# An attention layer in which the short operands of three kinds of products get zero rows up to 128

## The chip, the core and the metric

One Trainium2 chip, of which the kernel uses one core. The metric is the device time of one execution in microseconds (us); less is better. Engines are named as in the profile: PE is TensorE's matmul, PEld TensorE's weight load, DVE is VectorE, ACT ScalarE, POOL GpSimd, and SP the engine that issues most DMAs.

## What is computed

One inference step of a two-layer decoder for a prompt of 1024 tokens and eight sample sequences of four new tokens each. Layer 0 is a pooling and state-space mixer, layer 1 is attention; each layer ends with a SwiGLU feed-forward part. The change lies in layer 1's attention alone, cut here to what matters:

```python
DILATED_PATTERNS = ((128, 1), (512, 4), (2048, 16))   # (window, dilation)

def mixer_c_prompt(xn, w_qkv, w_o):                   # 1024 tokens, 16 heads of 64
    q, k, v = _split_qkv(xn, w_qkv)
    for window, dil in DILATED_PATTERNS:
        o, lse = dilated_branch_prompt(q, k, v, window, dil)
        ...
    y = _merge_patterns(outs, lses).reshape(b, t, ATT_WIDTH).astype(xn.dtype) @ w_o

def mixer_c_sample(xn, cache_k, cache_v, w_qkv, w_o): # 8 sequences, 4 tokens, 2048 cached rows
    q, k, v = _split_qkv(xn, w_qkv)
    kk = jnp.concatenate([cache_k, k.astype(cache_k.dtype)], axis=1)
    vv = jnp.concatenate([cache_v, v.astype(cache_v.dtype)], axis=1)
    for window, dil in DILATED_PATTERNS:
        idx = buf + jnp.arange(t)[:, None] - dil * jnp.arange(span + 1)[None, :]
        kg, vg = kk[:, idx], vv[:, idx]
        sc = jnp.einsum('bthe,btjhe->bhtj', q, kg, ...) * scale
        p, den, lse = _softmax_stats(sc, valid[None, None])
        o = jnp.einsum('bhtj,btjhe->bthe', p, vg.astype(jnp.float32)) / ...
```

The three patterns are merged into one softmax by the logarithm of the number of patterns that see a distance; that is the mask `strip` (prompt) and `smask` (sample).

## The kernel before

Everything is float32. Most products are made of parts: a value is split into a high part in the reduced type `F32R` and a low part, which is what the high part lacks, and a product is the sum of two or three products of parts (`mm3`, lines 170 to 173). An operand's rows are the partitions over which a product sums. The program is written as a long list of steps. In layer 0 and in the feed-forward parts a scheduler decides their order on each engine; in the two stages of the change (`with tc.manual_schedule()`, lines 1549 and 1933) the order is as written.

**Projections and cached keys (lines 1327 to 1577).** `Project` makes 128 columns of q, k or v from all tokens (lines 171 to 173, 8 times 3 products of 384 or 288 columns for each third of the tokens), and between its groups `keys_slot` handles the 56 tiles of cached keys that the samples look at. For 48 of these tiles `Keys.queries` (line 1453) brings one sample's query rows onto all partitions: two products of 512 columns each with a selector (`selq` or `selh`) as the stationary operand and `qh` as the moving one. `qh` has 64 rows: the high parts of the 32 query rows, then their low parts. ACT or DVE then take the result (lines 1469 and 1472), and POOL or DVE multiply it with the keys.

**Attention (lines 1582 to 1996).** 160 slots, ten for each of the 16 heads, go through a software pipeline that is written out by hand in the loop of line 1941. A slot's steps are:

- PE, `Row.scores` (lines 1838 and 1839): one or two blocks of scores, 128 queries against up to 512 keys. A head's 64 features lie on its own half of the partitions (`own`), and the low part of its queries on the other half (`oth`). The first product takes all 128 rows of `qs` (query high and low parts) against `kh` (the key's high part, on both halves). The second adds the key's low part and takes `own` alone: 64 rows of `qs` against 64 rows of `kl`. There are 12 such pairs in a head, 192 in all: 96 of 512 columns, and 32 each of 384, 256 and 128.
- DVE, `Row.masked` (line 1849): mask and running maximum from PSUM; ACT, `Row.exp` (line 1856), one slot later.
- PE, `Chunk.transposes` (line 1873), six slots after the scores; ACT, `Chunk.hi` (line 1883), and DVE, `Chunk.lo` (line 1890), copy the result into two parts.
- PE, `Chunk.values` (lines 1897 to 1905), two slots after that.
- ACT `fold`, DVE `scale` and `out`, POOL (line 154) at the end of a unit.
- Steps of `Sample`, one of the eight sequences every 20 slots: PE turns its scores and probabilities (lines 1702 to 1705 and 1729 to 1732), and multiplies the probabilities with 16 half tiles of cached values (`product`, lines 1787, 1793, 1794). The last half tile of each eight holds the four new value rows, and its operands have four rows (`rr = TS`): `sw`, and rows 0 to 3 of `hi` and `lo`. ACT and POOL make these parts in `piece` (lines 1772 and 1773, POOL by the helper of line 154).

The buffers between the engines: PSUM banks `s` (3), `pt` (2), `po` (2), `so` (1); SBUF tiles `ph` and `pl` (3 each), `qs`, `kh` and `kl` (2 each: one head is loaded during the other). SP issues all loads of this stage: five for a head (line 1604), and those of cached values (`vpiece`, lines 1650 to 1662), the new rows by line 1662.

Of the kernel before, what the change touches and what calls it, by code (L numbers as in the profile page):

```python
# [18 lines left out]
# order of the steps in the even and odd slots of layer 0's mixer  # L19
ORDER = ("inputs rotate out outputs turn states turn_u scan sums".split(),  # L20
         "inputs rotate mix0 mix1 outputs turn scan mix2 means split".split())
# pieces of the values of the sample, and units of the prompt's queries, whose products are in plain float32
PLAIN_V = (1, 5)
PLAIN_U = 3
P = 128
# [3 lines left out]
NB = 8  # L29
# [3 lines left out]
# token quarters as they are worked on: (first column, number of columns); the second and the last one are  # L33
# followed by the samples' tokens of two steps each
QUARTERS = ((0, 256), (256, 272), (528, 256), (784, 272))
# and their order in the last chunk of the hidden features
# [14 lines left out]
# cached and new positions that one position of the sample looks at  # L51
# [8 lines left out]
def step_kernel(ctx, tc, x_prompt, x_sample, state_pool, state_s5, cache_k, cache_v, norm_gains,  # L60
# [36 lines left out]
    def nm(s):  # L97
        uid[0] += 1
        return f"{s}_{uid[0]}"
# [4 lines left out]
    def linbank():  # L104
        """one bank for products, of the kinds that the phase has to spare"""
        b = banks[-1]
        if not b.kinds:
            return mmbank()
        b.turn += 1
        return dict(m=mmbank, p=tpbank, q=tqbank)[b.kinds[b.turn % len(b.kinds)]]()[:, 0:512]  # L110
# [23 lines left out]
    # ---------------------------------------------------------------- weights  # L134
# [40 lines left out]
    def lin_first(ws, x, consumes):  # L175
        """several output tiles with the token tiles outermost, for an x that is still being made"""
# [17 lines left out]
    # ---------------------------------------------------------------- norms  # L194
# [30 lines left out]
    class Whole:  # L225
        """the features of all tokens in one piece"""
# [13 lines left out]
    class Blocks:  # L240
        """The features as the right-hand sides of seven products of halves (Winograd's form of Strassen's
        algorithm): blocks of half of the features and a quarter of the tokens, for two pairs of quarters, the
        first and the third one, and the second and the last one. Most blocks lie where quarters of y were."""
# [64 lines left out]
    class Boundary:  # L308
        """end of one sub-layer and start of the next for one tile of tokens, in stages"""
# [53 lines left out]
    class Tiles:  # L363
        """takes token tiles as they come; the second half of one overlaps the first half of the next"""
# [72 lines left out]
    class YTiles(Scope):  # L437
        """high and low parts of the features: by quarters of the prompt's tokens, the samples' with the second"""
# [7 lines left out]
        def prompt(self, k, c0=0, c1=SEQ):  # L446
            """(columns of a range of the prompt's tokens, high part, low part)"""
# [6 lines left out]
    # ================================================================ layer 0, mixer  # L454
# [46 lines left out]
    # ---- S5 tables, spilled to DRAM per quarter of 8 groups  # L501
# [32 lines left out]
    # cos and sin of the angle  # L534
# [17 lines left out]
    # powers of lambda_bar, 0..8  # L552
# [27 lines left out]
    # unit phasors e^(i 8 theta 2^k)  # L580
# [9 lines left out]
    # f = (lambda_bar - 1) / lambda ; b_bar = f * b  # L590
# [20 lines left out]
    # bst = [re; im] of b_bar, bss = [im; re]  # L611
# [7 lines left out]
    # c stacks: c1 = [re; -im], c2 = [im; re], columns (g, i)  # L619
# [16 lines left out]
    # h0 of the sample group: h0 = [re; im], h0s = [-im; re], columns (b, g)  # L636
# [16 lines left out]
    for q in range(4):  # L653
# [5 lines left out]
        # V: lambda^(7 - s) b_bar, stacks along the state, columns (g, s, i)  # L659
# [13 lines left out]
        # W: c lambda^k, columns (g, k, i)  # L673
# [11 lines left out]
        # K[d] = Re(c lambda^d b_bar), transposed, with d_skip on d = 0  # L685
# [15 lines left out]
        # E[c] = e^(i 8 theta c), columns (g, c)  # L701
# [24 lines left out]
    # ---- pooling half  # L726
# [9 lines left out]
    class Pool:  # L736
        """a group of the pooling channels, in steps"""
# [11 lines left out]
        def states(self):  # L749
# [6 lines left out]
            # new rows of the buffers  # L756
# [11 lines left out]
        def sums(self):  # L768
            """window sums by doubling"""
# [14 lines left out]
        def means(self):  # L784
            """divide by the count, subtract u"""
# [1293 lines left out]
```

## Time and profile before

| | us |
|---|---|
| median of 3 runs | 2861.05 |
| lowest and highest of them | 2856.1, 2862.39 |
| span of the profiled execution (first to last instruction) | 2854.8 |
| PE busy in it | 2704.5 (95%) |
| DVE, ACT, POOL busy in it | 1705.0, 1125.9, 1406.6 |

No time is listed for the profiled execution beside its span, which is 6.25 us under the median of the runs. Busy shares are means over stages of very different kinds. Times in the views are us from the first instruction. A PE record starts when the product's first column enters, its end is modelled, and records overlap; the time from one start to the next is what a product takes from the engine. "issue" stands for idle time that ends without anything that the profile shows.

### The profile page before, as it was taken

What the parts mean: (1) busy time and instruction counts of PE and PEld (TensorE: products, weight loads), DVE (VectorE), ACT (ScalarE), POOL (GpSimd) and SP (SyncE); (2) the same over time, 40 slices, a digit from 0 to 9 for tenths busy, and PEclk for the clock granted to TensorE, in tenths of its full rate; (3) what the DMA queues carried; (4) which work ended last, traced back from release to release, by engine and by line L of the source; (5) the groups of instructions that cost most, each with busy time, mean ns of one, the idle gap of its engine ahead of it and who ended that gap; (6) DMA issues with size and microseconds to landing.
All of it is one profiled execution on the core that took longest, in us unless ns stands there. A gap on an engine that the chain in (4) does not pass through costs nothing.

```text
span 2854.8 us, 49751 instructions
## 1 busy us (share of the span) xinstructions
PE 2704.5 (95%) x19508; PEld 2525.9 (88%) x19508; DVE 1705.0 (60%) x3117; ACT 1125.9 (39%) x2053; POOL 1406.6 (49%) x998
## 2 busy tenths in 40 slices
PE   7598998999999999899999999999989999999998
PEld 6587997999999999898888666667989999999998
DVE  8777379755552555733333688885497555543555
ACT  4134364322223211523433677775553222233112
POOL 5954456554556443113553455555465545555440
PEclk9798999999999999999999999999989999999999
DMA  5263362222224222525876655554533221223223
GB/s 147 101 202 109 114 196 96 94 78 77 79 83 147 91 91 76 166 105 169 236 201 175 159 145 145 145 145 130 175 117 98 79 83 65 90 92 104 91 91 130
DMA packets 275662, 350.75 MB, mean 123 GB/s; under 512 B 44056, under 2 KB 208668, under 8 KB 275420
## 3 DMA queue, kind: packets, MB, share of 16 engines
q1 hardware_dynamic: 215252, 289.82, 33.9%
q10 hardware_dynamic: 59024, 53.55, 5.6%
q0 software_dynamic: 1152, 4.19, 0.4%
q8 instruction: 154, 2.52, 0.4%
q14 instruction: 80, 0.66, 0.1%
HBM read 268.29 MB, written 79.39 MB: 122 GB/s over the span
## 4 chain that ended last, share of the span: by engine, by line
PE 79%; DVE 9%; issue 5%; DMA 3%; ACT 2%; POOL 2%; SPq 1%; POOLq 0%; ACTq 0%; DVEq 0%
PE pp L172 9%; PE pp L171 9%; PE pp L173 9%; PE mm L171 7%; PE mm L172 7%; PE mm L173 7%; PE pt L1873 3%; PE s L1839 2%; PE tp L172 2%; PE tp L173 2%; PE tp L171 2%; PE tq L171 2%; PE tq L172 2%; PE tq L173 2%; PE s L1838 2%
## 5 line engine op out<-in xcount | busy, mean ns | idle before, releaser
L171 PE MATMUL pp<-blk,whi 128*128 128x272 f32 (+1 forms) x2240 | 638.2, 287 | 9.3 <-DVE ct L1172 6.7
L172 PE MATMUL pp<-blk,wlo 128*128 128x272 f32 (+1 forms) x2240 | 641.1, 288 | 1.9 <-DVE wlo L1141 1.9
L173 PE MATMUL pp<-blk,whi 128*128 128x272 f32 (+1 forms) x2240 | 638.6, 287 | 0.0
L142 POOL TENSOR_TENSOR wlo<-wraw,whi 128x1024 fp32r<-128x1024 f32 x102 | 246.0, 2420 | 575.4 <-ACT whi L141 552.4
L171 PEld LDWEIGHTS pp<-blk,whi 128*128 128x128 f32 x2240 | 425.5, 191 | 10.7 <-DVE ct L1172 7.1
L172 PEld LDWEIGHTS pp<-blk,wlo 128*128 128x128 f32 x2240 | 425.3, 190 | 2.3 <-DVE wlo L1141 2.3
L173 PEld LDWEIGHTS pp<-blk,whi 128*128 128x128 f32 x2240 | 425.5, 190 | 0.0
L1172 DVE TENSOR_TENSOR c<-pp,c 128x528 f32<-128x528 f32 (+1 forms) x308 | 201.7, 656 | 336.6 <-PE pp L173 331.5
L1141 POOL TENSOR_TENSOR wlo<-S,whi 128x1024 fp32r<-128x1024 f32 x90 | 220.6, 2451 | 361.3 <-ACT whi L1140 361.2
L141 ACT CAST whi<-wraw 128x1024 fp32r<-128x1024 f32 x126 | 131.0, 1053 | 363.9 <-PE mm L173 107.3
L1140 ACT CAST whi<-S 128x1024 fp32r<-128x1024 f32 x100 | 105.0, 1050 | 344.2 <-PE pp L173 313.1
L173 PE MATMUL mm<-hid,whi 128*128 128x256 f32 (+1 forms) x680 | 194.5, 286 | 8.1 <-POOL hid L1260 8.1
L171 PE MATMUL mm<-hid,whi 128*128 128x256 f32 (+1 forms) x680 | 197.9, 291 | 1.8 <-DVE yacc L1281 1.8
L172 PE MATMUL mm<-hid,wlo 128*128 128x256 f32 (+1 forms) x680 | 194.5, 286 | 0.0
L171 PE MATMUL mm<-y,whi 128*128 128x256 f32 (+1 forms) x576 | 167.6, 291 | 0.4 <-DVE s5o L1031 0.4
L173 PE MATMUL mm<-y,whi 128*128 128x256 f32 (+1 forms) x576 | 167.0, 290 | 0.0
L172 PE MATMUL mm<-y,wlo 128*128 128x256 f32 (+1 forms) x576 | 166.7, 289 | 0.0
L1281 DVE TENSOR_TENSOR yacc<-mm,yacc 128x272 f32<-128x272 f32 (+1 forms) x264 | 113.1, 430 | 81.5 <-PE mm L173 81.5
L171 PE MATMUL tp<-hid,whi 128*128 128x272 f32 x484 | 138.3, 287 | 0.0
L172 PE MATMUL tp<-hid,wlo 128*128 128x272 f32 x484 | 138.1, 286 | 0.0
L173 PE MATMUL tp<-hid,whi 128*128 128x272 f32 x484 | 137.6, 285 | 0.0
L173 PEld LDWEIGHTS mm<-hid,whi 128*128 128x128 f32 x680 | 128.6, 189 | 8.9 <-POOL hid L1260 8.9
(516 smaller groups left out, 7684.9 us busy)
## 6 DMA issues: line engine op xcount, KB each, us to landing
wraw<-in_ffn_w_gate_dram SPq DMA_DIRECT2D x52, 512.0 KB
hid<-hd SPq DMA_DIRECT2D x44, 528.0 KB
raw<-in_ffn_w_up_dram SPq DMA_DIRECT2D x44, 512.0 KB
wraw<-in_ffn_w_down_dram SPq DMA_DIRECT2D x44, 512.0 KB
hd<-c ACTq DMA_DIRECT2D x72, 264.0 KB
wraw<-in_ab_w_out_dram SPq DMA_DIRECT2D x24, 512.0 KB
wraw<-in_c_w_qkv_dram ACTq DMA_DIRECT2D x24, 512.0 KB
kt<-in_cache_k_dram SPq DMA_DIRECT2D x32, 384.0 KB
```

The costliest lines, as they stand in the source:

```text
L141: A.copy(hi[:rows], raw[:rows])
L142: lo_eng.tensor_tensor(lo[:rows], raw[:rows], hi[:rows].bitcast(F32), op=sub)
L171: T.matmul(ps, wh, xh, start=start, stop=False)
L172: T.matmul(ps, wl, xh, start=False, stop=False)
L173: T.matmul(ps, wh, xl, start=False, stop=stop)
L1140: A.copy(hi, src)
L1141: (V if early and src is S34 else G).tensor_tensor(lo, src, hi.bitcast(F32), op=sub)
L1172: plus = lambda o, ps, x: V.tensor_tensor(o, ps, x, op=add)
L1281: V.tensor_tensor(yo, ps[:, :n], yo, op=add)
L1838: T.matmul(ps[:, :n], h.qs[:, i * P:(i + 1) * P], h.kh[:, c0:c0 + n], start=True, stop=False)
L1839: T.matmul(ps[:, :n], h.qs[h.own, i * P:(i + 1) * P], h.kl[h.own, c0:c0 + n], start=False, stop=True)
L1873: T.transpose(pt[:, j, r * P:(r + 1) * P], self.u.rows[r].p[:, (self.j0 + j) * P:(self.j0 + j + 1) * P], ident)
```

## The change

Three pairs of operands get zero rows up to 128, and the products take all 128:

- **Low keys.** `kl` is no longer taken from a pool for each head: there are two fixed tiles `klow`, one for even and one for odd heads, whose other half is set to zero once, by POOL. The second product of a pair takes all rows of `qs` and `kl`; the query's low part meets zeros.
- **Selectors.** `selq`, `selh` and `qh` have 128 rows; rows 64 to 127 of `qh` are set to zero once, by DVE, and those of the selectors come out as zeros since the identity has none of its ones there.
- **The sample's four rows.** `sw` becomes one fixed tile of 128 rows, made zero once, of which four rows are written for each sequence; the half tile of values is set to zero by POOL before SP loads its four rows; ACT and POOL make the parts of all 128 rows.

```diff
-                A.copy(q, self.queries(selq[:, i - 1, b:b + 1].to_broadcast([64, P])))
+                A.copy(q, self.queries(selq[:, i - 1, b:b + 1].to_broadcast([P, P])))
...
-    selq = stg.pool.tile([64, TS, NB], F32R, name="selq")
-    V.tensor_tensor(selq.rearrange("p t b -> p (t b)"), ident[0:64, 0:32], ident[0:64, 32:64], op=add)
-    selh = stg.pool.tile([64, 2, NB, P], F32R, name="selh")
+    selq = stg.pool.tile([P, TS, NB], F32R, name="selq")
+    V.tensor_tensor(selq.rearrange("p t b -> p (t b)"), ident[:, 0:32], ident[:, 32:64], op=add)
+    selh = stg.pool.tile([P, 2, NB, P], F32R, name="selh")
...
-                      selq[:, t].bitcast(F32).unsqueeze(2).to_broadcast([64, NB, 64]))
-    qh = stg.pool.tile([64, DM], F32R, name="qh")
+                      selq[:, t].bitcast(F32).unsqueeze(2).to_broadcast([P, NB, 64]))
+    qh = stg.pool.tile([P, DM], F32R, name="qh")
+    V.memset(qh[64:128].bitcast(F32), 0.0)
...
-            self.qs, self.kh, self.kl = t("qs"), t("kh"), t("kl")
+            self.qs, self.kh, self.kl = t("qs"), t("kh"), klow[a]
...
+    klow = [ap_.tile([P, SEQ], F32R, name=nm("kl")) for _ in range(2)]
+    for a, t in enumerate(klow):
+        G.memset(t[64 - 64 * a:128 - 64 * a].bitcast(F32), 0.0)
...
+        w = sc["sw"] = ap_.tile([P, P], F32R, name="sw")
+        V.tensor_scalar(w, ident, 0.0, None, op0=mult)
...
+                G.memset(dst, 0.0)
                 nc.sync.dma_start(dst[0:TS], dram_ap(vsd, b * TS * DM + c * 512, [[DM, TS], [1, 512]]))
...
-            sw = ap_.tile([4, P], F32R, name=nm("sw"), tag="sw", bufs=1)
+            sw = sc["sw"]
...
-            rr = TS if i % 8 == 7 else P
             cc = slice(u * 512, u * 512 + 512)
-            A.copy(hi[:rr, cc], raw[:rr, cc])
-            psub(lo[:rr, cc], raw[:rr, cc], hi[:rr, cc].bitcast(F32))
+            A.copy(hi[:, cc], raw[:, cc])
+            psub(lo[:, cc], raw[:, cc], hi[:, cc].bitcast(F32))
...
-            T.matmul(self.po, st, hi[:rr, cs], start=i % 8 == 0, stop=False)
-            T.matmul(self.po, st, lo[:rr, cs], start=False, stop=i % 8 == 7)
+            T.matmul(self.po, st, hi[:, cs], start=i % 8 == 0, stop=False)
+            T.matmul(self.po, st, lo[:, cs], start=False, stop=i % 8 == 7)
...
-            T.matmul(ps[:, :n], h.qs[h.own, i * P:(i + 1) * P], h.kl[h.own, c0:c0 + n], start=False, stop=True)
+            T.matmul(ps[:, :n], h.qs[:, i * P:(i + 1) * P], h.kl[:, c0:c0 + n], start=False, stop=True)
```

On PE both programs have the same instructions; in the two stages they stand in the same order, as do SP's in the whole program. What is added stands on POOL and DVE. POOL where the first sequence's four new value rows are split (`wlo`, `whi`: the low and high part of a piece, `wraw` or `vraw` the piece as loaded, `vst` and `v` a head's values, `vrh` their source, `y` a unit's result), before:

```order
L154 TENSOR_TENSOR wlo_16332<-wraw_16253,whi_16331 128x512 x2
L1611 COPY v_2388_16238<-vrh_16244 128x2x64
L154 TENSOR_TENSOR vst_16362<-vrh_16244,vst_16362 128x4x64 x2
L154 TENSOR_TENSOR wlo_16406<-vraw_16262,whi_16405 128x512 x2
L1611 COPY v_2389_16239<-vrh_16411 128x2x64
L154 TENSOR_TENSOR wlo_16464<-wraw_16358,whi_16463 128x512
L154 TENSOR_TENSOR vst_16436<-vrh_16411,vst_16436 128x4x64
L154 TENSOR_TENSOR wlo_16464<-wraw_16358,whi_16463 4x512
```

The same place in the changed program:

```order
L154 TENSOR_TENSOR wlo_16337<-wraw_16257,whi_16336 128x512 x2
L1669 MEMSET wraw_16362 128x512
L1613 COPY v_2389_16242<-vrh_16248 128x2x64
L154 TENSOR_TENSOR vst_16367<-vrh_16248,vst_16367 128x4x64 x2
L154 TENSOR_TENSOR wlo_16411<-vraw_16266,whi_16410 128x512 x2
L1613 COPY v_2390_16243<-vrh_16416 128x2x64
L154 TENSOR_TENSOR wlo_16469<-wraw_16362,whi_16468 128x512
L154 TENSOR_TENSOR vst_16441<-vrh_16416,vst_16441 128x4x64
L154 TENSOR_TENSOR wlo_16469<-wraw_16362,whi_16468 128x512
```

The new memset follows directly on the split of the piece that held the buffer before, and the last row has 128 rows in place of 4. DVE where the selectors are made, at the start of the projections, in the changed program:

```order
L1499 MEMSET qz 128x512
L1502 TENSOR_REDUCE selw<-ident 32x8
L1504 TENSOR_TENSOR selq<-ident 128x32
L1510 MEMSET qh 64x1024
L1507 CAST selh<-selq 128x8x64 x3
L165 TENSOR_TENSOR x2l<-tq_12992,x2h 128x8x128
```

Before, the memset of `qh` is not there and the selectors' rows read 64; the rest is the same.

## Rows read from the trace of the kernel before

**Rows 1.** The page's head and its first part: span, then busy time of each engine, its share of the span and its instructions.

```profile
span 2854.8 us, 49751 instructions
...
PE 2704.5 (95%) x19508; PEld 2525.9 (88%) x19508; DVE 1705.0 (60%) x3117; ACT 1125.9 (39%) x2053; POOL 1406.6 (49%) x998
```

**Rows 2.** Busy time by stretch: the projections with the cached keys (1300 to 1575 us), and two stretches of 50 us of attention. After the stretch stand its length and each engine's busy time with its instructions, in the order PE, PEld, DVE, ACT, POOL, then the granted clock of TensorE as a share of full speed, the DMA engines' busy share and GB/s.

```profile
1300.00:1575.00 275.00, 268.36 (x1588) 242.95 (x1588) 95.46 (x108) 106.44 (x135) 131.13 (x57) 0.97 0.70 199
1675.00:1725.00 50.00, 50.00 (x274) 34.76 (x273) 40.80 (x129) 37.53 (x99) 29.10 (x34) 1.00 0.55 143
1775.00:1825.00 50.00, 50.00 (x273) 34.79 (x272) 40.24 (x125) 37.30 (x98) 28.27 (x32) 1.00 0.58 149
```

**Rows 3.** Instructions of one source line, by line (1838, 1839 and 1453): count, shortest, median and longest record in ns, first and last start, shapes (rows*columns of the stationary operand, then moving operand). The row "issue" belongs to line 1839: how long its engine, PEld's part of it, sat idle before it, and how often.

```profile
L1838 PE MATMUL s<-kh,qs x192: 218/387/798, 1575.2 to 1953.3; 128*128 128x512 f32 x96, 128*128 128x128 f32 x32, 128*128 128x256 f32 x32, 128*128 128x384 f32 x32
...
L1839 PE MATMUL s<-kl,qs x192: 322/490/792, 1575.4 to 1954.0; 64*128 64x512 f32 x96, 64*128 64x128 f32 x32, 64*128 64x256 f32 x32, 64*128 64x384 f32 x32
...
  issue: 49.9, 137
...
L1453 PE MATMUL tp<-qh,selq x64: 383/395/498, 1317.7 to 1563.6; 64*128 64x512 f32 x64
...
L1453 PE MATMUL tp<-qh,selh x32: 387/393/501, 1333.4 to 1569.8; 64*128 64x512 f32 x32
```

**Rows 4.** PE's timeline at three places of attention: start, length, engine, line, operation, operands, rows*columns of the stationary operand, moving operand, count.

```profile
1790.45 0.33 PE L1839 MATMUL s<-kl,qs 64*128 64x128 f32 x1
1790.70 0.38 PE L1838 MATMUL s<-kh,qs 128*128 128x256 f32 x1
...
1794.35 0.28 PE L1905 MATMUL po<-pl,vst 128*128 128x256 f32 x1
1794.46 0.39 PE L1793 MATMUL so<-whi,z 128*128 128x512 f32 x1
1794.70 0.40 PE L1794 MATMUL so<-wlo,z 128*128 128x512 f32 x1
1794.93 0.39 PE L1838 MATMUL s<-kh,qs 128*128 128x512 f32 x1
1795.25 0.49 PE L1839 MATMUL s<-kl,qs 64*128 64x512 f32 x1
1795.67 0.66 PE L1873 MATMUL pt<-ident,Pr 128*128 128x128 f32 x4
...
1796.53 0.28 PE L1905 MATMUL po<-pl,vst 128*128 128x256 f32 x1
1796.74 0.49 PE L1793 MATMUL so<-whi,sw 4*128 4x512 f32 x1
1797.07 0.39 PE L1794 MATMUL so<-wlo,sw 4*128 4x512 f32 x1
1797.39 0.30 PE L1702 MATMUL s<-ident,sN 128*64 128x128 f32 x1
```

**Rows 5.** PE's timeline around one pair of selector products in the projections, same columns.

```profile
1568.98 0.34 PE L172 MATMUL tq<-x2h,wlo 128*128 128x384 f32 x1
1569.15 0.34 PE L173 MATMUL tq<-x2l,whi 128*128 128x384 f32 x1
1569.42 0.73 PE L1453 MATMUL tp<-qh,selh 64*128 64x512 f32 x2
1570.08 0.40 PE L171 MATMUL mm<-x2h,whi 128*128 128x288 f32 x1
1570.32 0.30 PE L172 MATMUL mm<-x2h,wlo 128*128 128x288 f32 x1
1570.46 0.29 PE L173 MATMUL mm<-x2l,whi 128*128 128x288 f32 x1
```

**Rows 6.** Who waited for whom, in attention (1575 to 1975 us; the first three rows) and in the projections (1310 to 1575 us; the other two): us in total, times, longest.

```profile
ACT ph L1883 <- PE pt L1873: 81.1, 124, 3.6
...
DVE Pr L1849 <- PE s L1839: 42.5, 46, 2.2
DVE pl L1890 <- ACT ph L1883: 30.1, 68, 1.1
...
PEld mm L171 <- issue: 8.4, 23, 0.4
...
PEld tq L171 <- issue: 4.7, 13, 0.4
```

**Rows 7.** Groups of instructions by line and shape, in attention (the first four) and in the whole program (memsets): count, then busy time in us and mean ns of one, then the idle time before them.

```profile
L154 POOL TENSOR_TENSOR wlo<-wraw,whi 128x512 fp32r<-128x512 f32 x53 | 67.6, 1278 | 61.2 <-ACT whi L1772 55.8 <-issue 2.3 <-DMA vraw<-in_cache_v_dram 1.2
...
L1772 ACT CAST whi<-wraw 128x512 fp32r<-128x512 f32 x53 | 32.4, 611 | 0.1
...
L154 POOL TENSOR_TENSOR wlo<-wraw,whi 4x512 fp32r<-4x512 f32 x11 | 14.1, 1283 | 0.6 <-ACT whi L1772 0.3
...
L1772 ACT CAST whi<-wraw 4x512 fp32r<-4x512 f32 x11 | 6.8, 615 | 0.1
...
L734 POOL MEMSET counts<- 128x1 f32 x16 | 0.6, 98 | 7.3 <-DVE vb L671 7.3
...
L1621 POOL MEMSET v<- 128x128 f32 x2 | 0.3, 205 | 3.6 <-DVE pr L1472 3.6
...
L967 DVE MEMSET usm<- 40x1024 f32 x1 | 0.9, 912 | 0.2 <-issue 0.2
```

More of the change, by code (lines that the diff above doesn't have):

```diff
@@ L1745, in place @@
             tmp = ap_.tile([P, 2, 16], F32, name=nm("tmp"), tag="tmp", bufs=1)
-            self.parts = [(sn[:, 0:64], sn[:, 64:128], pn[:, 0:64]), (sw[:, 0:64], sw[:, 64:128], pn[0:4, 192:256]),
+            self.parts = [(sn[:, 0:64], sn[:, 64:128], pn[:, 0:64]), (sw[0:4, 0:64], sw[0:4, 64:128], pn[0:4, 192:256]),
                           (diag(0, P, 0, 144, 4), diag(0, P, 64, 144, 4), far),
@@ L1782, in product @@
                 self.po = bank("so", 1)
-            rr = TS if i % 8 == 7 else P
             cs = slice(u * 512, u * 512 + 512)
-            st = self.st[i % 8][:rr]
+            st = self.st[i % 8]
             if j in PLAIN_V:
-                T.matmul(self.po, st.bitcast(F32), vpieces[idx][:rr, cs], start=i % 8 == 0, stop=i % 8 == 7)
+                T.matmul(self.po, st.bitcast(F32), vpieces[idx][:, cs], start=i % 8 == 0, stop=i % 8 == 7)
                 if u:
```

## Prediction

> **What bounds the kernel.** The page comes first: PE is busy for 2704.5 of 2854.8 us [rows 1], so time on PE is time of the kernel wherever PE never waits. The busy time by stretch says where that is, and how near the next engine stands: in attention PE is busy for 50.00 us of 50, DVE for 40.2 to 40.8, ACT for 37.3 to 37.5, POOL for 28 to 29 [rows 2]; in the projections PE is busy for 268.4 of 275, and no other engine for half of it. Both stages are PE's, but in attention DVE stands right behind. The rows by source line give the number of short products: 192 of 64 rows in attention (line 1839) and 64 + 32 = 96 in the projections (line 1453) [rows 3]; the sample's four-row products are two in each of 16 half tiles. They also show something odd: ahead of line 1839's weight loads PEld sat idle 137 times, 49.9 us in all, for no reason that the profile shows ("issue"). The timeline says what that is.
>
> **What a short product costs.** Read PE's timeline from start to start. Among products of 128 rows, 512 columns take 0.24 us (1794.46 to 1794.70 to 1794.93) [rows 4]. Then come the scores: from line 1838 (128 rows) to line 1839 (64 rows) 0.32 us, from line 1839 to the transposes 0.42 us, with no wait named, and at a granted clock of 1.00, the 2.4 GHz level, all through [rows 2]. So going from 128 rows to 64 costs 0.08 us, and the short product itself, up to the next of 128 rows, 0.18 us. The second cost does not hang on the width: the short product of 128 columns takes 0.25 us (1790.45 to 1790.70), more than one of 512 columns and 128 rows. After a change of rows, the next gap is also long: in the projections the first product of 288 columns after a selector pair takes 0.24 us, the second 0.14 [rows 5]. I read all of this as one thing: PE overlaps a product and the next weight load only while the number of rows stays the same.
>
> **Attention, on PE.** Each of the 192 pairs sheds 0.08 + 0.18 = 0.26 us: 49.9 us. The first step after it is a transpose for most; for a matmul it would be 0.10 us shorter [rows 5], for a transpose no row shows it. Bounds are 0 and 0.10; I take the middle, 0.05: 9.6 us (0 to 19). The sample's four rows: 0.21 us from line 1905 into them where 0.11 is normal, 0.33 for the first instead of 0.24, 0.32 for the second instead of 0.24 [rows 4], 0.27 together; 16 times that is 4.3 us, less about half of the last term, since every second time 64-row transposes follow that stay as they are: 3.7. Sum 63 us (54 to 73).
>
> A rule stands against this. The Trainium skill, "TensorE: Matmul & The Clock Gate", section "Why this matters for your kernels", says that a single product of 32 rows takes the same time as one of 128, the gain of fewer rows being that several can run at once. By it the sum for padding would be 0. The trace does not agree: 0.42 us against 0.24 at equal width, though the rule speaks of a product alone and these stand between products of 128 rows.
>
> **Attention, what is late next.** The 160 slots run from 1575.2 to 1953.3, 378 us [rows 3]. PE alone would then need 378 - 63 = 315. DVE needs 40.8 / 50 x 378 = 308, ACT 37.5 / 50 x 378 = 284 [rows 2]. DVE's long waits in the stage are 42.5 us for the scores and 30.1 us for ACT's copy of the transposes, and ACT in turn waited 81.1 us for the transposes [rows 6]: all 72.6 us go back to PE, so they can shrink with it, but no more than 72.6 can come off before DVE never rests. Three engines would then be within a tenth of each other, tied by two or three buffers. If the pace were PE's alone, 63 us are saved. If DVE kept its waits for ACT, whose own share rises from 75% to about 86%, only the 42.5 us for the scores could go; losing a little more to uneven slots, 36 us is my lower end. I take 4% over PE's 315, because the two-slot lag of the values and the three score banks let a heavy slot of one engine lie beside a light one of another: 328 us, **50 us saved** (36 to 70; the upper end is the 73 held back by DVE's 308).
>
> **Projections.** A pair of selector products: 0.27 us from line 173 into it where 0.17 is normal, 0.66 for the two where twice 0.24 is 0.48, and 0.24 for the next product instead of 0.14 [rows 5]: 0.38 us for a run. The 96 products make at most 48 runs; PEld's unexplained idle time behind them was met 23 + 13 = 36 times [rows 6], since some pairs adjoin. 36 to 48 runs give 14 to 18 us. DMA is busy for 0.70 of this stretch [rows 2], and key tiles, POOL's products and DVE's sums are chained through four buffers; so I count **12 us** (6 to 18).
>
> **What is added.** POOL gets two memsets of 1024 columns and 16 of 512. From 98 ns for one column and 205 for 128 [rows 7] I estimate 0.53 us for 512 and 0.96 for 1024: 10 us over a stage in which POOL is busy for 29 of 50. The two for `klow` come while the last projections still run, and `v`'s memsets behind them waited 3.6 us there anyway. In `vpiece` the memset stands right behind the split that frees the buffer; behind it on POOL wait a head's values and the next piece, both slots ahead of their use. SP's load of the four rows now waits for it, but SP first issues two loads of the same piece; queued behind on SP are the next pieces and a head's five loads, which are needed nine slots later. DVE's memset of `qh` costs at most the 0.91 us of a like one [rows 7], at the start of the projections where DVE is busy for a third; zeroing `sw` once is less. ACT and POOL take 128 rows instead of 4 at the same price: 615 and 611 ns, 1283 and 1278 ns [rows 7]. All of this I count at nothing; if POOL's cover were gone in attention it would be 10 us, and PE would have to wait for POOL first. In the last feed-forward part the scheduler exchanges a few products and their sums, in kind and number the same: nothing.
>
> **Sum.** 50 + 12 = 62 us. The profiled span of 2854.8 becomes 2793; the median of the runs lies 6.25 us over that span, and I carry that over: 2861 - 62 = **2799 us**.
>
> **Rivals.**
> - *DVE and ACT take over early.* For: three engines at 75% and more; slots differ in kind, and a wait of DVE for ACT is a matter of order, not of PE's speed. Against: the score banks let PE run ahead. Then attention saves 15 to 30 us and the projections 6 to 12: 2819 to 2840. Chance 0.15.
> - *PE keeps the whole gain.* DVE, fed in time, follows PE: 63 to 70 and 16 us, 2775 to 2782. For: DVE's 308 us are under PE's 315. Chance 0.10.
> - *Rows do not matter.* The delay would sit in the operands' place or in the second weight load of a pair, and padding changes nothing: 2861. Against: lines 1793 and 1794 also add a second product to the same bank, at 0.24 us, and at four rows the same two lines take 0.33 and 0.32. Chance 0.04. The rule of the Trainium skill's TensorE page above would give this too.
> - *Slower: short products share the array.* If line 1839's product now ran beside its neighbours on the half that they leave free, a padded one would add its own passage: 96 x 0.24 us for 512 columns and 32 each of 0.17 [rows 5], 0.11 [rows 4] and a quarter of 0.24 for 384, 256 and 128, 34 us in all: 2895. It decides where a short product's time to the next start lies under that of 128 rows, 0.24 us at 512 columns; the rows have 0.42 there, and the selector pairs 0.33 each. It could hold only for parts that these rows do not show. Chance 0.04. The Trainium skill, "TensorEngine Tiling (Array Packing)", section "When to Use Tiling", recommends tiling for a sum over 64 rows and so argues for keeping the rows short; no row here shows two short products on different halves side by side.
>
> **How the numbers follow.** The forecast has 0.67, the rivals 0.15, 0.10, 0.04 and 0.04. The range takes the forecast's ends, 36 + 6 = 42 us and 70 + 16 = 86 us saved, and the greater part of the first rival: 2775 to 2832. A measurement of this kernel tells about 0.2%, 6 us, from no change. Faster by more: 0.67 + 0.15 + 0.10, of which I give 0.01 up for a gain that is lost elsewhere: 0.91. Within it: 0.04 + 0.01 = 0.05. Slower: 0.04.
>
> **What would show it.** In the changed profile, the gap from the first to the second score product and from that to the transposes should both be near 0.24 us at 512 columns, and "issue" ahead of the second weight load gone. 160 slots should take about 328 us, with DVE near 94% busy and DVE's waits for the scores mostly gone; new waits of PE for DVE's release of the score banks would then be the next bound. The projections should be about 12 us shorter at the same count of products. It is wrong if the gaps stay above 0.4 us (rows do not matter), if attention stays over 350 us (DVE and ACT), or if PE or SP comes to wait for POOL's memsets.

## The result, and the profile after

| | before | changed |
|---|---|---|
| median of 4 runs | 2859.82 us | 2787.69 us (2785.69 to 2790.38) |
| ratio | | 0.9748 [0.9736, 0.9761], 72.1 us less |
| span of the profiled execution | 2854.8 us | 2783.9 us |
| projections: first selector product to first score product | 257.5 us | 238.4 us |
| attention: first to last score product | 378.1 us | 329.0 us |
| before the projections; after attention | 1317.7; 901.5 us | 1315.1; 901.4 us |

The kernel is 2.5% faster; 2799 us was forecast, and the range held the time. The last three lines split the 70.9 us between the spans: 49.0 in attention (first to last means the start of the first and of the last pair of score products), 19.1 in the projections, 2.6 ahead of them, where the program is unchanged. The page of the changed kernel, for [rows 1]: PE has as many instructions as before and 86.5 us less to do.

```profile
span 2783.9 us, 49802 instructions
...
PE 2618.0 (94%) x19508; PEld 2518.7 (90%) x19508; DVE 1701.7 (61%) x3119; ACT 1122.9 (40%) x2053; POOL 1423.2 (51%) x1016
```

For [rows 2], two stages of the changed kernel and 50 us out of the second; columns as there.

```profile
1315.10:1553.50 238.40, 230.27 (x1474) 222.84 (x1473) 93.28 (x106) 98.69 (x126) 130.00 (x58) 0.99 0.79 220
1553.50:1882.50 329.00, 313.97 (x1976) 258.46 (x1977) 302.17 (x940) 275.30 (x712) 218.78 (x252) 0.98 0.64 163
1653.00:1703.00 50.00, 48.31 (x313) 40.08 (x312) 47.11 (x144) 42.62 (x110) 34.66 (x42) 1.00 0.61 159
```

The same two stages of the kernel before:

```profile
1317.70:1575.20 257.50, 250.86 (x1472) 225.81 (x1473) 91.36 (x102) 98.47 (x125) 127.81 (x56) 0.97 0.73 204
1575.20:1953.30 378.10, 374.09 (x1981) 256.92 (x1978) 296.42 (x942) 278.50 (x712) 209.57 (x236) 0.98 0.55 142
```

Attention's PE time falls by 60 us (374.1 to 314.0), the stage by 49: PE goes from 99% busy to 95%. DVE is busy for 92% of the stage, and for 47 us of the 50 in the third line. In the projections PE's busy time falls by 21 us (250.9 to 230.3), and the granted clock rises from 0.97 to 0.99; the second was in no step of the prediction.

For [rows 4], PE's timeline in the changed kernel (line 1844 is the high product of the scores, before 1838; line 1845 the low one, before 1839; 1879 the transposes, before 1873):

```profile
1772.77 0.39 PE L1799 MATMUL so<-whi,sn 128*128 128x512 f32 x1
1773.00 0.40 PE L1800 MATMUL so<-wlo,sn 128*128 128x512 f32 x1
1773.23 0.39 PE L1844 MATMUL s<-kh,qs 128*128 128x512 f32 x1
1773.46 0.40 PE L1845 MATMUL s<-kl,qs 128*128 128x512 f32 x1
1774.13 0.55 PE L1879 MATMUL pt<-ident,Pr 128*128 128x128 f32 x3 [0.27 <-DVE pl L1896]
```

Read from start to start: 0.23 us for each of the four 512-column products up to 1773.46, where the low one cost 0.42. What stands behind it now is a wait with a name: the transposes start 0.67 us later, and 0.27 of it PE waits for DVE. This is one place; what follows is read from all pairs of 512 columns that ran at the full clock. From the low product to the transposes the median is 0.23 us, where it was 0.43. From the high to the low product it hangs on what stands ahead of the pair: 0.23 instead of 0.32 behind the low part of a value product, as here (30 pairs before, 31 now), and as the median of all pairs 0.34 instead of 0.43. Pair by pair, and without those that now wait, padding took away 0.09 us on the way into the low product, 0.20 on the way out and 0.06 at the step behind. For [rows 3], line 1845 in the changed kernel, with PEld's unexplained idle time:

```profile
L1845 PE MATMUL s<-kl,qs x191: 274/390/628, 1554.5 to 1880.9; 128*128 128x512 f32 x95, 128*128 128x128 f32 x32, 128*128 128x256 f32 x32, 128*128 128x384 f32 x32
...
  issue: 8.6, 33
```

"Issue" there is 8.6 us in 33 places, where it was 49.9 in 137. For [rows 6], the waits of attention (us in total, times, longest):

```profile
ACT ph L1889 <- PE pt L1879: 36.6, 69, 1.6
...
DVE pl L1896 <- ACT ph L1889: 11.8, 33, 0.8
...
DVE Pr L1855 <- PE s L1845: 6.9, 11, 1.9
PEld s L1844 <- DVE mxp L1855: 6.7, 9, 0.8
...
PE s L1844 <- DVE mxp L1855: 5.3, 8, 0.7
```

ACT's wait for the transposes is halved (81.1 to 36.6), DVE's for the scores is 6.9 instead of 42.5, and PE and PEld now wait for DVE's release of a score bank (5.3 and 6.7 us, which partly lie side by side). The queue is turned round: DVE waited for PE, now each waits a little for the other.

### The profile page after: what moved, and what is told of

Read it like the earlier page. It is cut to its first block, busy times and chain, and to the rows that moved or that the text cites. A ratio compares the mean times of both kernels' runs of the same rounds, so it can differ in the third digit from the quotient of the medians.

```text
span 2783.9 us, 49802 instructions
## 1 busy us (share of the span) xinstructions
PE 2618.0 (94%) x19508; PEld 2518.7 (90%) x19508; DVE 1701.7 (61%) x3119; ACT 1122.9 (40%) x2053; POOL 1423.2 (51%) x1016
## 4 chain that ended last, share of the span: by engine, by line
PE 70%; DVE 12%; POOL 6%; DMA 4%; issue 4%; ACT 3%; SPq 1%; ACTq 0%; DVEq 0%; POOLq 0%
PE pp L172 9%; PE pp L171 9%; PE pp L173 9%; PE mm L171 7%; PE mm L172 6%; PE mm L173 6%; PE tp L172 2%; PE tp L171 2%; PE tp L173 2%; PE tq L171 2%; PE tq L172 2%; PE tq L173 2%; POOL e L529 2%; PE pt L1879 1%; POOL es L529 1%
## 5 line engine op out<-in xcount | busy, mean ns | idle before, releaser
L1141 POOL TENSOR_TENSOR wlo<-wraw,whi 128x512 fp32r<-128x512 f32 (+1 forms) x56 | 117.8, 2103 | 36.0 <-ACT whi L1140 36.0
```

What stands on the lines that cost most here:

```text
L1141: (V if early and src is S34 else G).tensor_tensor(lo, src, hi.bitcast(F32), op=sub)
```

## The experiments

Every kernel was timed in four runs or more, and its ratio goes by the kernel before as timed beside it (median 2859.82 us for the changed kernel, 2856.58 for e1 to e4, 2859.99 for e5 to e8, 2857.55 for e10 to e13). "Stage" is attention from the first score product's start to the last one's in the profiled execution. Since the half-clock stretch at the stage's start has another length and place in each, the last column is used to compare them: from the start of the 25th pair of score products to the last one's, which lies behind that stretch.

| kernel | median us, ratio [95%] | projections | stage | 25th to last |
|---|---|---|---|---|
| before | | 257.5 | 378.1 | 329.2 |
| changed | 2787.69, 0.9748 [0.9736, 0.9761] | 238.4 | 329.0 | 288.9 |
| e1 low keys alone | 2804.91, 0.9821 [0.9798, 0.9843] | 261.2 | 324.2 | 282.9 |
| e2 selectors alone | 2840.38, 0.9944 [0.9927, 0.9960] | 240.9 | 377.8 | 329.2 |
| e3 four rows alone | 2855.34, 0.9989 [0.9979, 1.0000] | 261.4 | 374.1 | 325.5 |
| e4 before, short product twice | 2895.95, 1.0138 [1.0117, 1.0158] | 261.1 | 413.8 | 359.7 |
| e5 changed, cast on POOL | 2788.95, 0.9745 [0.9724, 0.9765] | 239.3 | 322.3 | 282.0 |
| e6 changed, more plain products | 2794.53, 0.9763 [0.9742, 0.9784] | 242.4 | 333.9 | 292.4 |
| e7 changed, memset four times | 2795.82, 0.9772 [0.9758, 0.9787] | 239.9 | 333.8 | 294.1 |
| e8 changed but for the four rows | 2782.28, 0.9725 [0.9711, 0.9738] | 239.9 | 323.2 | 283.0 |
| e10 e8, cast on POOL | 2785.49, 0.9743 [0.9720, 0.9766] | 239.8 | 323.4 | 282.9 |
| e11 changed, again | 2786.42, 0.9748 [0.9726, 0.9769] | 241.9 | 329.5 | 288.9 |
| e12 changed, fill by DMA | 2789.95, 0.9759 [0.9737, 0.9781] | 240.2 | 332.9 | 289.2 |
| e13 e12, cast on POOL | 2782.24, 0.9734 [0.9715, 0.9754] | 241.4 | 322.4 | 279.4 |

### Is it the change of the row count, or the short product itself?

**e4** is the kernel before with the low product issued twice:

```diff
+            T.matmul(ps[:, :n], h.qs[h.own, ...], h.kl[h.own, ...], start=False, stop=False)
             T.matmul(ps[:, :n], h.qs[h.own, ...], h.kl[h.own, ...], start=False, stop=True)
```

> The kernel before with each short score product (line 1839) issued twice, one right behind the other, so that the low key counts twice in the scores. Theory: the change of rows costs and the short product does not, so the second one adds the passage of a product of its width alone, 96 x 0.24 + 32 x (0.17 + 0.11 + 0.06) = 34 us: 2894 us, and the gap from the first to the second short one is longer than normal while the gap out of the second is as the gap out of the one before. Rival, every short product takes 0.42 us by itself: 96 x 0.42 + 32 x (0.37 + 0.31 + 0.25) = 70 us more, 2930.

The stage grew by 35.7 us, where 34 were expected by the theory and 70 by the rival. PE's timeline in e4: high product, short, short, transposes.

```profile
1796.09 0.50 PE L1838 MATMUL s<-kh,qs 128*128 128x512 f32 x1
1796.52 0.50 PE L1839 MATMUL s<-kl,qs 64*128 64x512 f32 x1
1796.86 0.39 PE L1840 MATMUL s<-kl,qs 64*128 64x512 f32 x1
1797.18 0.66 PE L1874 MATMUL pt<-ident,Pr 128*128 128x128 f32 x4
```

The stage in e4, in the columns of [rows 2]:

```profile
1575.60:1989.40 413.80, 410.39 (x2171) 279.20 (x2169) 296.46 (x943) 278.53 (x712) 209.97 (x236) 0.98 0.51 130
```

From the first short product to the second 0.34 us, from the second to the transposes 0.32: together 0.66, 0.24 more than the 0.42 of one. The medians over all such pairs are the same to 0.01. The second one thus costs no more than a product of 128 rows; what a short product costs beyond that is paid once, for going there and back. The theory had one detail wrong: it left the gap out of the last short product at 0.42, and it is 0.32. The rival by which short products share the array falls with it too. The Trainium skill, "TensorEngine Tiling (Array Packing)", section "Key Properties", says that changing the tiling mode drains TensorE. These rows fit it, with 0.24 us as the price, if an operand of 64 rows is such a mode; no run here shows that it is.

### The three parts apart

**e1** (low keys):

```diff
-            self.qs, self.kh, self.kl = t("qs"), t("kh"), t("kl")
+            self.qs, self.kh, self.kl = t("qs"), t("kh"), klow[a]
...
+    klow = [ap_.tile([P, SEQ], F32R, name=nm("kl")) for _ in range(2)]
+    for a, t in enumerate(klow):
+        G.memset(t[64 - 64 * a:128 - 64 * a].bitcast(F32), 0.0)
...
-            T.matmul(ps[:, :n], h.qs[h.own, ...], h.kl[h.own, ...], start=False, stop=True)
+            T.matmul(ps[:, :n], h.qs[:, ...], h.kl[:, ...], start=False, stop=True)
```

> The kernel before with the low keys alone padded (192 products of line 1839). Theory: PE loses time only where the number of rows changes from one product to the next, and attention is now held by DVE close behind PE. PE sheds 59 us of 378, DVE holds some of it back, so the stage goes to about 332 us and the whole to about 2814 us (2808 to 2820); the projections stay at their length. Rival, each part counts for itself without DVE in the way: 59 us come off, 2801. Rival, the selectors and the four rows made most of the gain: 2840 or more.

Its projections, then its attention:

```profile
1317.90:1579.10 261.20, 254.19 (x1472) 228.87 (x1472) 92.17 (x104) 98.85 (x126) 129.76 (x58) 0.95 0.72 201
1579.10:1903.40 324.30, 315.59 (x1978) 258.52 (x1978) 294.48 (x942) 275.86 (x712) 210.72 (x236) 0.98 0.65 165
```

PE shed 58.5 us in attention against 59.5 forecast (49.9 + 9.6), and the stage came to 324.3: 8 us shorter than the 332 of the theory, by which DVE holds more of the gain back, and shorter than with the whole change. So something in the rest of the change costs some 6 us there (last column, 282.9 against 288.9).

**e2** (selectors):

```diff
-    selq = stg.pool.tile([64, TS, NB], F32R, name="selq")
+    selq = stg.pool.tile([P, TS, NB], F32R, name="selq")
...
-    qh = stg.pool.tile([64, DM], F32R, name="qh")
+    qh = stg.pool.tile([P, DM], F32R, name="qh")
+    V.memset(qh[64:128].bitcast(F32), 0.0)
```

> The kernel before with the selectors and qh alone padded (96 products of line 1453). The stage of the projections became 19 us shorter in the changed kernel, where 0.38 us for each of 36 to 48 runs of short products give 14 to 18. Theory: the rows give 15 us, 2845 us in all, and the other 4 us were TensorE's granted clock, 0.97 before and 0.99 after in that stage. Rival, all 19 us come from the rows: 2841.

16.2 us less by the medians, and 16.6 us less from the first selector product to the first score. The projections of e1, e3 and e4, which keep the 64-row selectors, are no shorter than before (261.1 to 261.4), so all of the stage's gain comes from this part. The time does not tell the theory (15 us less) from the rival (19 less): the interval runs from 11 to 21. The clock and the products do. Granted clock (third number from the end) by 50 us, before, changed, and e2:

```profile
1350.00:1400.00 50.00, 49.99 (x302) 44.58 (x301) 17.16 (x20) 21.50 (x27) 31.00 (x14) 1.00 0.76 220
1400.00:1450.00 50.00, 48.88 (x296) 44.18 (x296) 20.04 (x26) 18.88 (x23) 26.77 (x12) 0.97 0.81 235
1450.00:1500.00 50.00, 48.92 (x280) 44.70 (x279) 14.06 (x16) 19.65 (x25) 24.46 (x11) 0.93 0.65 182
1500.00:1550.00 50.00, 50.00 (x300) 45.39 (x299) 16.68 (x18) 19.76 (x25) 17.50 (x8) 0.97 0.71 196
```

```profile
1350.00:1400.00 50.00, 50.00 (x320) 48.82 (x320) 21.57 (x26) 22.28 (x29) 35.47 (x15) 1.00 0.87 245
1400.00:1450.00 50.00, 48.68 (x326) 47.04 (x326) 17.37 (x23) 21.41 (x27) 28.43 (x13) 1.00 0.90 255
1450.00:1500.00 50.00, 48.73 (x318) 47.46 (x316) 17.40 (x18) 20.51 (x27) 21.75 (x10) 1.00 0.73 198
1500.00:1550.00 50.00, 49.47 (x315) 47.67 (x315) 19.36 (x21) 20.66 (x26) 26.12 (x14) 1.00 0.66 181
```

```profile
1350.00:1400.00 50.00, 49.96 (x321) 48.29 (x320) 17.69 (x21) 21.22 (x28) 33.23 (x14) 1.00 0.82 224
1400.00:1450.00 50.00, 48.67 (x327) 46.96 (x326) 20.57 (x27) 20.60 (x26) 28.48 (x12) 1.00 0.90 259
1450.00:1500.00 50.00, 48.73 (x315) 47.36 (x313) 18.80 (x20) 22.38 (x29) 23.03 (x10) 1.00 0.70 195
1500.00:1550.00 50.00, 49.47 (x316) 47.73 (x315) 15.47 (x17) 21.36 (x27) 24.63 (x11) 1.00 0.71 194
```

In the kernel before, three of the four slices lie at 0.93 to 0.97; in the changed one and in e2 all four stay at 1.00. By the clock's records, the time at the half level (1.2 GHz) within the projections is 17.1 us before and 23.9 in each of e1, e3 and e4; with 128-row selectors it is 3.4 to 6.8 in all ten profiled executions. What it costs can be read twice: products of 384 columns go from 0.18 to 0.32 us apart, 0.44 us for each us at the half level; and e1, e3 and e4 have 6.8 us more of it than before and a stage 3.6 to 3.9 longer, 0.55 for each. The 13.7 us that the change takes away are then worth 6 to 7.5. The trace can also be read product by product, since the 1472 products of the stage stand in the same order in both kernels: from start to start, those into, between and just behind selector products lost 14.6 us where both kernels ran at the full level, products at which either kernel was at the half level lost 6.1, and longer waits took 1.7 back. **So of the 19.1 us, about 6 are the clock's and 14.6 the rows', less 1.7 for waits.** In e2 the same three numbers are 14.4, 2.7 and 0.7: the theory's 15 us and its clock term, and not the rival. The kernel before falls to the half level five times. At 1345.3 PE is in a wait of 3.4 us for a key tile's DMA, and the changed kernel falls behind the same wait, at 1342.1. The other four falls come 0.9 to 1.8 us behind the start of a 64-row selector pair; ahead of the pair PE had run 16 products of 8 columns (three times) or waited 1.1 us (once). The changed kernel runs the same 16 products and then the padded pair, and stays at the full level. Whether the stalls of the pair or its 64 rows decide it was not tried apart.

**e3** (four rows):

```diff
+        w = sc["sw"] = ap_.tile([P, P], F32R, name="sw")
+        V.tensor_scalar(w, ident, 0.0, None, op0=mult)
...
+                G.memset(dst, 0.0)
...
-            sw = ap_.tile([4, P], F32R, name=nm("sw"), tag="sw", bufs=1)
+            sw = sc["sw"]
...
-            rr = TS if i % 8 == 7 else P
+            rr = P
```

> The kernel before with the sample's four-row operands alone padded (32 products in 16 pairs). Theory: 3.7 us less, 2856 us, by 0.1 us into a pair, 0.1 in it and 0.08 out of it where what follows has 128 rows. Rival, pairs of four rows hardly cost anything since they follow each other: 0 to 1 us less. Rival, the added memsets and longer parts on POOL hold PE up: slower than before.

Its attention:

```profile
1578.90:1953.00 374.10, 370.08 (x1979) 256.76 (x1977) 301.93 (x943) 278.75 (x712) 217.56 (x252) 0.98 0.56 143
```

PE shed 4.0 us against 3.7 forecast, and the stage is 4.0 shorter: where PE bounds the stage, the price is right and nothing stands against it. In the time it is not told from no change.

### What bounds attention now?

**e5** takes a cast (`y<-yt`, line 1933) from DVE to POOL; **e6** takes split work off DVE and gives PE the products in plain float32.

```diff
-            V.tensor_copy(hi, self.yt[h.own])
+            G.tensor_copy(hi, self.yt[h.own])
```

> The changed kernel (2788 us) with the copy of a unit's high part (DVE's cast y<-yt, 64 times) made by POOL instead of DVE. Theory: DVE bounds attention in the changed kernel, and part of it is this cast, which takes 0.28 us alone and 1.06 us where POOL works beside it, 36 us in all; without it PE's 314 us bound the stage, which goes from 329 to about 318 us, 2777 in all, and the cast on POOL takes some 0.45 us. Rival, PE bounds the stage already and the rest of its idle time is order: no change, 2785 to 2790. Rival, POOL gets too much: slower than the changed kernel.

The stage in e5:

```profile
1564.10:1886.40 322.30, 312.87 (x1978) 258.83 (x1978) 268.12 (x882) 276.45 (x712) 240.02 (x311) 0.98 0.65 166
```

The edit of e6:

```diff
-            self.direct = j0 == 0 and unit.ip == PLAIN_U
+            self.direct = j0 == 0 and unit.ip in (1, 2, 3)
```

> The changed kernel with the first chunk of three units of a head in plain float32 instead of one (32 chunks more), which takes their low part (0.69 us each on DVE, 22 us in all) away and two passes of 256 columns on PE for the two products of parts (0.22 against 0.24 us each). Theory, DVE bounds attention: the stage goes from 329 to about 316 us, 2775 in all. Rival, PE bounds it: within 3 us of the changed kernel.

The stage in e6:

```profile
1561.10:1895.00 333.90, 324.57 (x1976) 267.51 (x1977) 282.32 (x909) 275.34 (x710) 218.60 (x252) 0.98 0.63 161
```

e6 relieved DVE by 20 us and cost PE 10.6, and the stage became 4.9 longer. If DVE set the pace it would have come to about 316 us, so that theory falls. But the stage grew by less than PE's work did: PE's time without work fell from 15.0 to 9.3 us. e5 relieved DVE by 34 us, and the stage lost 6.7, down to PE at 97% and 9.4 us without work. **So PE's work bounds the stage, and some 6 us on top of it come from DVE being late.** The median of e5 did not fall with its stage: in the profiled execution, the projections began at 1324.8 us instead of 1315.1, which more than takes the 6.7. That execution is the longest of its four runs (2778.2 to 2791.6 us). Over all the kernels that start lies between 1310.3 and 1324.8, though the edits lie behind it; why is open.

### What do the four rows cost, now that PE is faster?

**e8** is the changed kernel without that part (e1 and e2 together), **e7** the changed kernel with four memsets in place of one, **e11** the changed kernel once more:

```diff
 # e7
                 G.memset(dst, 0.0)
+                G.memset(dst, 0.0)
+                G.memset(dst, 0.0)
+                G.memset(dst, 0.0)
```

> The kernel before with low keys and selectors padded, the sample's four rows as before. Theory: padding the four rows sheds 4 us on PE but makes DVE's casts longer (mean 0.49 us with the low keys alone, 0.57 with all three), and DVE bounds: without it attention takes 324 us as with the low keys alone, and the whole about 2783, 4 to 5 us less than the changed kernel. Rival, each part of the change helps: 2791.

> The changed kernel with each of the 16 memsets of a half tile of values issued four times (25 us more on POOL, which is busy for 219 of 329 us in attention). Theory: POOL's work lengthens DVE's casts that meet it, and DVE is the bound: some 10 us slower than the changed kernel, 2798 (2792 to 2808), with the mean cast well over its 0.57 us. Rival, as the prediction had it, memsets on POOL cost nothing: 2788.

> The changed kernel as it is, once more, so that the other kernels of this call stand beside it on the same chip. 2786 to 2790 us; attention 329 us, the mean cast 0.57 us.

e8's attention:

```profile
1555.90:1879.20 323.30, 314.85 (x1978) 257.89 (x1978) 293.86 (x941) 275.08 (x712) 210.76 (x236) 0.99 0.65 166
```

Though PE has 0.9 us more to do than in the changed kernel, the 25th-to-last part is 283.0 instead of 288.9 us; e1 has 282.9, and the changed kernel again 288.9. Stage and median (323.2 and 2782.28 us) are those that were expected. In the medians the difference is 4 to 5 us, less than the intervals can tell apart. **In attention, padding the four rows costs 6 us once the low keys are padded.** The groups of instructions name DVE's cast (count, then busy us and mean ns of one), changed, then e8:

```profile
L1933 DVE CAST y<-yt 64x256 fp32r<-64x256 f32 x64 | 36.6, 572 | 1.3
...
L1669 POOL MEMSET wraw<- 128x512 f32 x11 | 5.8, 526 | 0.7
```

```profile
L1931 DVE CAST y<-yt 64x256 fp32r<-64x256 f32 x64 | 31.4, 491 | 1.3
```

The cast takes 5.2 us longer in all, the size of what is lost. It works on tiles that neither part touches. The timeline shows what it meets. In e8, where POOL splits a four-row piece (line 154, `wlo`):

```profile
1639.57 1.28 POOL L154 TENSOR_TENSOR wlo<-wraw,whi 4x512 fp32r<-4x512 f32 x1
...
1640.11 0.90 DVE L1931 CAST y<-yt 64x256 fp32r<-64x256 f32 x1
...
1640.82 0.78 POOL L154 TENSOR_TENSOR vst<-vrh,vst 128x256 fp32r<-128x256 f32 x1
...
1641.68 0.73 POOL L154 TENSOR_TENSOR y<-yt,y 64x256 fp32r<-64x256 f32 x1
...
1644.82 0.27 PE L1843 MATMUL s<-kl,qs 128*128 128x128 f32 x1
1645.05 0.50 PE L1842 MATMUL s<-kh,qs 128*128 128x512 f32 x1
```

and in the changed kernel, at the same step of a later sequence:

```profile
1679.77 1.28 POOL L154 TENSOR_TENSOR wlo<-vraw,whi 128x512 fp32r<-128x512 f32 x1
...
1680.31 1.59 DVE L1933 CAST y<-yt 64x256 fp32r<-64x256 f32 x1
...
1681.01 0.73 POOL L154 TENSOR_TENSOR vst<-vrh,vst 128x256 fp32r<-128x256 f32 x1
...
1682.04 0.74 POOL L154 TENSOR_TENSOR y<-yt,y 64x256 fp32r<-64x256 f32 x1 [0.30 <-DVE y L1933]
...
1684.97 0.28 PE L1845 MATMUL s<-kl,qs 128*128 128x128 f32 x1
1685.94 0.50 PE L1844 MATMUL s<-kh,qs 128*128 128x512 f32 x1 [0.69 <-DVE mxp L1855]
```

Both casts start 0.54 us into POOL's split, which takes 1.27 to 1.28 us in both. Beside four rows the cast lasts 0.90 us and ends 0.16 behind the split; beside 128 rows it lasts 1.59 and ends only behind the next operation of POOL too. Alone it takes 0.27 to 0.29. In the changed kernel DVE then works without a rest up to the end of the lines shown, and these tell what becomes of the 0.69 us: the same score product starts 4.94 us behind the cast in e8 and 5.63 behind it in the changed kernel, where PE waited 0.69 us for DVE's release of the score bank.

The 64 casts stand in the same order in both kernels. Eight are at this step, one in each sequence: seven go from 0.90 to 1.60 us, and that of the last sequence, which starts just ahead of the split, from 0.29 to 1.46. Seven others start 0.24 us into the same kind of split and take 1.2 us in both kernels, and seven that met other work of POOL in e8 are 0.13 shorter. From one score product to the next, the changed kernel falls behind e8 in the same steps in each of the seven sequences of the last part: 0.70 us at the product shown, 0.5 in two waits of transposes for DVE's `pl`, and 0.33 won back at the padded products. That is 0.85 for a sequence and 5.9 in all.

The Trainium skill, "GPSIMD Engine Reference", section "8. Key points", says that POOL shares its SBUF interfaces with VectorE. The rows agree: wherever a split lengthens the cast, it ends 0.15 to 0.16 us behind the end of an operation of POOL. Which one differs: behind a split of four rows it is that split, behind one of 128 rows at this offset the next operation, though POOL's own times are the same. Why the cast passes the end of the split is not settled, and ACT's copy, which got its 128 rows together with POOL's split, was not tried apart.

e11, the changed kernel again, gave 2786.42 us and 329.5 for the stage, so the stage repeats to 0.5 us. e7 adds three memsets of 0.53 us to each of 16 pieces, and the last part grows by 5.2 us to 294.1; the casts are then at 632 ns in the mean, and the median, 2795.82 us, lies in the range that was expected. Memsets thus can cost, so **e12** fills the buffer by a transfer of cache rows in its place, and **e13** and **e10** take the cast off DVE in e12 and e8:

```diff
 # e12
-                G.memset(dst, 0.0)
+                near_rows(cache_v, b, 0, dst, 0, c)
```

> The changed kernel, all three parts padded, but instead of POOL's memset a DMA of 128 rows of the cache goes into the half tile before the four new rows overwrite its first ones; what lies in rows 4 to 127 is multiplied with zeros. 16 loads of 256 KB more, 16 memsets less on POOL. Theory: the changed kernel lost in attention because the memsets hold DVE's casts up; without them the mean cast is back at 0.49 us and the stage at 319 to 323 us, as without the four rows or less: 2780. Rival: it is not the memsets but the order in which POOL now works; no change, 2788. Rival: SP waits longer in line, slower.

> As the one before, with the copy of a unit's high part on POOL as well. Theory: attention is bound by PE alone, 312 us of work, and takes 316 to 320 us: 2777. Rival: the two gains are the same gain (both take DVE's cast out of POOL's way): as the better one alone, 2780.

> The kernel before with low keys and selectors padded, the four rows as before, and the copy of a unit's high part on POOL. Theory: with the cast off DVE and no memsets, PE is the bound at 97% and more of attention, 314 us of work: the stage takes 319 to 321 us (323 with the cast on DVE, 322 with the cast on POOL and all three parts), and the whole some 3 us less than without the move, 2779. Rival: POOL's copy, 0.4 us, makes the low part and the values later and costs what DVE gains: 2782.

The casts of e12:

```profile
L1933 DVE CAST y<-yt 64x256 fp32r<-64x256 f32 x64 | 36.6, 571 | 1.3
```

Without the memset they are as long as with it, and the last part is 289.2: the one memset is not the cause, and the theory that it was falls. Taking the cast off DVE then saves 9.8 us in that part (e12 to e13), 6.9 in the changed kernel (e5), and 0.1 in e8 (e10). The cast's place on DVE costs something just where the four rows are padded. Neither e13 nor e10 came down to the stage that was expected with PE alone as the bound (316 to 321 us): they have 322.4 and 323.4. e8 and e13 have the lowest medians, 5 us under the changed kernel's; their intervals overlap with its, so neither is shown to beat it.

## Why the prediction was right, and where not

- **A change of row count costs 0.26 us and up, at full clock.** Right: pairs of 512 columns lost 0.09 us into the short product and 0.20 out of it, "issue" fell from 49.9 to 8.6 us, and e4 shows that the price hangs on the change. The 0.32 us into the short product was read at one place; elsewhere it is 0.43 to 0.73, but padding took the same 0.09 off. That PE no longer overlaps a product and a weight load is how the prediction reads the gaps; the runs show the gaps and PEld's idle time, not the reason. The Trainium skill's rule on one product of 32 rows ("TensorE: Matmul & The Clock Gate", section "Why this matters for your kernels"), which was weighed against the row, does not hold between products of 128 rows: 0.43 us there, 0.23 when padded.
- **PE sheds 63 us in attention.** 60 by the busy time; 58.5 (forecast 59.5) by e1 and 4.0 (3.7) by e3. The middle taken for the step behind a short product, 0.05 us, is 0.06 in the trace.
- **The stage at 328 us.** 329.0, but for a wrong reason in part, and that the two lie so near is luck. The 4% over PE's time were put down to uneven slots of three engines. e1 and e8 have 324 and 323 us, 2.7% over PE's time; the rest is the next point.
- **"ACT and POOL take 128 rows instead of 4 at the same price", counted at nothing.** This step failed. The price of the operations is the same, 1.28 us, but eight casts of DVE beside them become 0.7 to 1.2 us longer, PE waits for the DVE that is late by it, and the stage becomes 6 us longer. It is the term that a row of durations can't show. The memset, also counted at nothing, shows no cost of its own (e12).
- **Projections, 12 us.** 19.1. The rows alone are 14.6 us, within the 14 to 18 that were added up (there are 40 runs); the part taken off it for other engines and the DMA was too large, as longer waits took 1.7. The term that lacks is the clock, about 6, which the 0.97 of [rows 2] had in it unread.
- **Rivals.** "DVE and ACT take over early" fell: 49 us were saved, not 15 to 30, and by e5 and e6 DVE's lateness is some 6 us of the stage. "PE keeps the whole gain" (2775 to 2782) is what e8 comes near, 2782.3, without the part that hurts DVE. "Rows do not matter" and "short products share the array" fell with the gaps and with e4.
- **The sum** was 62 us and came to 72.1: 1 less in attention, 7 more in the projections, 2.6 from time ahead of them that is not the change's, and 1.2 by which the medians differ more than the two profiled spans.

## What to carry to other kernels

Look for products of fewer rows between products of 128: where the gap behind them is longer than the columns explain and the profile names no wait, pad the rows, or put the short ones next to each other, since only the change costs. Before padding, ask for each operand which other engine's operations grow in rows with it, and who works beside those: an operation of the same duration can still hold up a neighbour. Read the granted clock of a stage as a term of its own, since a stage without stalls may also get a higher one.

## What the runs showed that I had not expected

- A DVE cast of 64x256 from SBUF to SBUF takes 0.28 us alone, 0.90 when it starts 0.54 us into a POOL split of 4 rows and 1.59 at the same place in one of 128 rows; 0.24 us into either split it takes 1.2.
- In the projections, 17.1 to 23.9 us at half clock with 64-row selectors (four executions) and 3.4 to 6.8 with 128-row ones (ten), without an exception.
